# Four edits to the order of work in a hybrid encoder step: low halves, head operands, seven-product jobs, first gate

## The chip, the cores and the metric

The kernel runs on one core of a Trainium2 chip, as one launch. The metric is the device time of that launch in microseconds (us), less is better. The engines are named as in the profile: PE is TensorE (matmuls, PEld its weight loads), DVE is VectorE, ACT is ScalarE, POOL is GpSimd, SP is SyncE, whose queue issues nearly all DMAs.

## The reference, cut to what matters

One layer over 512 prompt tokens and 64 sample tokens. The normalised input is projected by one wide matrix into eleven pieces of 1024 columns, which feed three branches: a gated recurrence (A), differential attention (B) and attention into 256 memory tokens (M). Each branch output is gated, projected again, and the three are merged by sigmoid gates that come from the same first projection.

```
xn = rms_norm(x, g_norm)
hq, hf, hi, za, dq, dk, dv, zb, mq, zm, gr = split_columns(xn @ w_in)
...                       # y_a: recurrence, y_b: differential attention, y_m: memory attention
gates = sigmoid(gr).reshape(B, T, 3, D_MODEL)
h = 0
for n, (y_n, z_n) in enumerate(((y_a, za), (y_b, zb), (y_m, zm))):
    h = h + gates[:, :, n] * ((y_n * silu(z_n)) @ w_branch[n])
y = x + h @ w_out
```

## The kernel before, in words

**Products.** Every projection is done in pieces of 256 output columns, called jobs. A float32 product is made of three fp32r products: weights and tokens are each split into a high half (a copy in fp32r, made by ScalarE) and a low half (the rest, a subtraction), and high x high, high x low and low x high are added up in PSUM. A job comes in three kinds. "N" puts tokens on the rows of the result (`mms`, L333 for the prompt, L346 for the sample). "T" puts output columns on the rows (`mms`, L297): four groups of 24 matmuls of 288 tokens, 96 in all. "S" (`strassen`, L460) gives the same result as "T" from seven block products in place of eight, 84 matmuls; for that it needs sums of weight blocks (L249, VectorE), seven split units of weights where the others have four, and sums of partial results (L425, L433 on VectorE, L440 on ScalarE).

**Weights.** `load_next` issues the DMA of half a job's weights into one of three `raw` buffers (L187, SP). `conv_next` issues the splits in the order of `plan`: the high half on ScalarE (L215), the low half (L218) on the engine that `lo_engine` names. Until the sums of S jobs exist (`XS`, made at the end of the recurrence) every second low half of T and N jobs goes to POOL, 44 in all; later all go to VectorE. Eight units of split weights are kept (`NUNIT`), and units are converted while the job before runs.

**The order of the work** is written by hand. `seq` lists the jobs; `run_jobs` walks through them, and after each 12 matmuls or so calls `weave`, one step of the clock by which everything else is issued: `later(n, fn)` runs `fn` n steps on, and each generator that was pushed (`push(gen, rate)`) advances by `rate` pieces per step. Every engine takes its instructions in the order in which they were issued, so a wait holds all that stands behind it.

- `rest` (L1921 on) normalises and transposes the input blocks beside the first job: `prep_x` scales a block, `prep_xT` transposes it on TensorE (L618) and splits it (L622, L625; for the sample also `xs2`, L628, L629).
- `hgrn` is the recurrence of one head: scans and reciprocals on VectorE, products on VectorE and POOL (L835, `Kb` among them), then small matmuls (L912 to L971).
- `mem_head` is the memory attention, and `diff_pair` the differential attention of two heads. Its table `todo` puts pieces on steps: for head j, with `y0` 0 or 14, the operands `build_q`, `build_k`, `build_s` at steps `y0`, `y0 + 1`, `y0 + 2` (transposes L1115, high halves L1125 and L1142, low halves L1129 and L1145, copies to the other 64 rows L1146 and L1147), score products (L1204, L1205, then maximum L1212 and exponential L1220) from `y0 + 5`, then `combine`, `transp` (L1243, L1246) and `values` (L1276). Pairs 0 to 2 run at rate 1, the last at `LAST_B` = 1.5. `finish_heads` then normalises, transposes (L768, after L759) and gates a head; `y_out` stores it, `y_splits` loads it again and splits it (L675, L679) for the branch projection.
- `gr_jobs(n)` are the gate jobs of branch n, S jobs whose tanh (L1682) is stored to DRAM (`g_store`). `branch_jobs(n)` project a branch's heads (T jobs). Branch 0 stores its result to DRAM (`r_d`). Branch 2 loads that, its own gate and gate 0, applies gate 0 (L1709) and adds its own gated result (L1707, L1711); branch 1 does the same with the sum and gate 1, and splits the result for the last projection.

**`seq` from the pairs on**, before the change: `dq`, `dk` (N) of pair 0; `dv`, gate, `z` (S) of pair 0, gate; pair 1's three N jobs; then the two S jobs `z` of pairs 1 and 2 side by side; pair 2's three N jobs; the S job `z` of pair 3 and the last gate job `gr[11]` side by side; pair 3's three N jobs; branch 2; branch 1; the last projection. Pair 2 is pushed with `z` of pair 3, pair 3 with branch 2. The first job of branches 2 and 1 begins with the heads that are there and waits for the rest; heads of branch 1 are split only while about `spare` slots or more are free, and branch 2's slots are given back at the start of branch 1 (`y_free(2)`).

Of the kernel before, what the change touches and what calls it, by code (L numbers as in the profile page):

```python
# [66 lines left out]
def encoder_step(ctx, tc, ins, outs):  # L67
# [99 lines left out]
    lo_n = [0]  # L167

    def lo_engine():

        lo_n[0] += 1
        return ge if lo_n[0] % 2 == 0 and not XS else ve
# [311 lines left out]
    def later(n, fn):  # L484

        due.setdefault(tick[0] + n, []).append(fn)
# [616 lines left out]
    def diff_pair(hp, A):  # L1103
# [177 lines left out]
        for j, y0 in ((0, 0), (1, 14)):  # L1281
            for d, fn in enumerate((build_q, build_k, build_s)):
                todo.setdefault(y0 + d, []).append((4, fn, (j,)))
            for i in range(NT + 1):
                for rank, (d, fn) in enumerate(((D_VAL, values), (D_TR, transp), (D_COMB, combine), (0, lambda j, i: scores(j, i, 0)),
                                                (1, lambda j, i: scores(j, i, 1)))):
                    todo.setdefault(y0 + 5 + 2 * i + d, []).append((rank, fn, (j, i)))
# [357 lines left out]
    g0 = {}  # L1645
    r_d = [drams.tile([P, TT], F32, name=f"r_{b}") for b in range(8)]
    h_d = {n: [drams.tile([P, TT], F32, name=f"h{n}_{b}") for b in range(8)] for n in (2,)}
    g_d = {n: [drams.tile([P, TT], F32, name=f"g{n}_{b}") for b in range(8)] for n in range(3)}
# [19 lines left out]
    def gr_jobs(n):  # L1668

        out = []  # L1670
        for c in range(4):
            def dst(blk, half, c=c):
                b = 2 * c + blk
                if b not in gates:
                    gates[b] = slots.get()
                return gates[b][:, half * TH : (half + 1) * TH]

            def evac(blk, half, src, c=c, dst=dst):
                b = 2 * c + blk
                sl = slice(half * TH, (half + 1) * TH)  # L1680
                g = dst(blk, half)
                se.activation(out=g, in_=src, func=AF.Tanh, scale=0.5)  # L1682
                seen[b] = seen.get(b, 0) + 1
                if seen[b] == 2:
                    seen.pop(b)
                    later(2, lambda: g_store(n, b))
            seen = {}
            j = Job(w_in, GR + n * D + c * CW, "S", evac, f"gr{n}")
            j.dst = dst
            out.append(j)  # L1690
        return out

    def branch_jobs(n):
        out = []
        for c in range(4):
            def evac(blk, half, ps, c=c):
# [11 lines left out]
                if n == 2 and half == 0:  # L1708
                    ve.scalar_tensor_tensor(out=h2[b][:, 0:TT], in0=g0[b][:, 0:TT], scalar=1.0, in1=h2[b][:, 0:TT], op0=ALU.add, op1=ALU.mult)  # L1709
                    slots.put(g0.pop(b))  # L1710
# [20 lines left out]
            if n:  # L1731
                def pre(c=c):
                    def load(b):
                        h_load(h_d[2] if n == 1 else r_d, b)
                        gates[b] = g_load(n, b)
                        if n == 2:
                            g0[b] = g_load(0, b)
                    if c == 0:
                        load(0)
                    load(2 * c + 1)  # L1740
                    if c < 3:
                        later(5, lambda: load(2 * c + 2))
                before(j, pre)
# [47 lines left out]
    LAST_A, LAST_B = 1.1, 1.5  # L1791
# [41 lines left out]
    gr = gr_jobs(0) + gr_jobs(2) + gr_jobs(1)  # L1833
# [38 lines left out]
    seq += [DJ[0][2], gr[9], DJ[0][3], gr[10]] + DJ[1][0:3] + [DJ[1][3], DJ[2][3]] + DJ[2][0:3] + [DJ[3][3], gr[11]] + DJ[3][0:3]  # L1872
# [4 lines left out]
    seq += br  # L1877
    br = branch_jobs(1)
    br[0].gate = lambda: None
    before(br[0], lambda: y_free(2))  # L1880
# [10 lines left out]
    with tc.manual_schedule():  # L1891
# [24 lines left out]
        def rest():  # L1916
# [8 lines left out]
            yield  # L1925
            prep_xT(3)
            yield
            yield
            prep_xT(4)
            put(*gn)  # L1930
            yield
# [37 lines left out]
```

## Time and profile before

| | |
|---|---|
| median of 3 runs | 1121.91 us (1118.06 to 1123.19) |
| the profiled execution | 1122.42 us |
| its span, first to last instruction | 1120.7 us |
| TensorE's mean granted clock | 0.992 |
| ACT busy, POOL busy | 573.3 us, 233.4 us |
| HBM read, written | 114.74 MB, 34.47 MB |

A row of busy time by stage holds: from and to, length, then for each engine its busy time and number of instructions, TensorE's granted clock, the busy share of the DMA engines and GB/s. A row of waits holds: who waited (engine, tile, line), who ended it, the total, how often, the longest. A piece of the chain holds its start, its length and what it was. A row of a group holds the line, engine, operation, tiles, shapes and number, then busy time and the mean of one in ns, then the idle time before it. Line numbers are those of the kernel before.

### The profile page before, as it was taken

How to read it: one execution, taken by the hardware profiler on the slowest of the kernel's cores; microseconds unless marked ns; L12 is line 12 of the kernel's file. 1: busy time of each engine (PE TensorE's matmuls, PEld its weight loads, DVE VectorE, ACT ScalarE, POOL GpSimd, SP SyncE). 2: the span in 40 equal slices, each digit the busy share in tenths (PEclk: the TensorE clock that was granted, in tenths of full speed). 3: DMA queues.
4: the chain of work that ended last, by engine and by line, in shares of the span. 5: the costliest groups of instructions: out<-in, count | busy, mean ns of one | idle time of the engine just before them, and what ended most of it. 6: DMA issues, size and time to landing. Idle time of an engine off the chain costs nothing.

```text
span 1120.7 us, 22273 instructions
## 1 busy us (share of the span) xinstructions
PE 1091.1 (97%) x8685; PEld 1073.7 (96%) x8685; DVE 789.9 (70%) x1603; ACT 573.3 (51%) x1355; POOL 233.4 (21%) x406
## 2 busy tenths in 40 slices
PE   8999999999999999999999999999998998899998
PEld 6999999999899999999999999998998998898998
DVE  5479495876835666688784679679769878776641
ACT  6443323333233466568675557757757855643220
POOL 2435455453610000000000210140221131010000
PEclk9999999999999999999999999999999999999999
DMA  5442233224323656754435333223223536465442
GB/s 190 151 147 71 78 102 96 63 85 130 121 93 120 216 192 205 226 191 157 145 120 185 102 121 112 74 96 114 66 80 115 174 102 225 165 215 183 145 141 65
DMA packets 127930, 150.66 MB, mean 134 GB/s; under 512 B 7731, under 2 KB 104655, under 8 KB 127825
## 3 DMA queue, kind: packets, MB, share of 16 engines
q1 hardware_dynamic: 127820, 149.24, 41.2%
q8 instruction: 68, 1.11, 0.4%
q14 instruction: 38, 0.30, 0.1%
q10 hardware_dynamic: 4, 0.00, 0.0%
HBM read 114.74 MB, written 34.47 MB: 133 GB/s over the span
## 4 chain that ended last, share of the span: by engine, by line
PE 81%; DVE 9%; DMA 3%; ACT 3%; issue 2%; POOL 1%; SPq 1%; DVEq 0%; ACTq 0%; POOLq 0%
PE d L297 26%; PE d L333 25%; PE d L460 14%; PE d L346 4%; DVE wl L218 3%; PE abank L1276 1%; DMA raw<-in_w_in_dram 1%; PE abank L1530 1%; DVE slot L249 1%; PE abank L1243 1%; PE abank L912 1%; PE abank L1597 1%; PE abank L1205 1%; ACT wh L215 1%; PE abank L948 1%
## 5 line engine op out<-in xcount | busy, mean ns | idle before, releaser
L333 PE MATMUL d<-wh,xh 128*128 128x256 f32 x768 | 223.4, 291 | 0.8 <-ACT xh L622 0.8
L333 PE MATMUL d<-wh,xl 128*128 128x256 f32 x768 | 218.4, 284 | 0.5 <-DVE xl L625 0.3
L333 PE MATMUL d<-wl,xh 128*128 128x256 f32 x768 | 218.2, 284 | 0.0
L218 DVE TENSOR_TENSOR wl<-raw,wh 128x512 fp32r<-128x512 f32 x240 | 171.8, 732 | 54.2 <-ACT wh L215 52.8
L215 ACT ACTIVATE wh<-raw 128x512 fp32r<-128x512 f32 x284 | 168.2, 622 | 4.8 <-DMA raw<-in_w_in_dram 4.4
L297 PE MATMUL d<-slot,wh 128*128 128x288 f32 x768 | 159.3, 301 | 3.6 <-DVE slot L679 3.5
L333 PEld LDWEIGHTS d<-wh,xh 128*128 128x128 f32 x768 | 147.9, 193 | 2.0 <-ACT xh L622 1.2
L333 PEld LDWEIGHTS d<-wh,xl 128*128 128x128 f32 x768 | 147.9, 193 | 1.0 <-DVE xl L625 1.0
L333 PEld LDWEIGHTS d<-wl,xh 128*128 128x128 f32 x768 | 148.2, 193 | 0.5
L460 PE MATMUL d<-XS,wh 128*128 128x288 f32 x640 | 132.7, 301 | 0.0
L297 PEld LDWEIGHTS d<-slot,wh 128*128 128x128 f32 x768 | 126.0, 192 | 5.5 <-DVE slot L679 4.6
L297 PE MATMUL d<-xh,wh 128*128 128x288 f32 x384 | 116.7, 304 | 0.0
L297 PE MATMUL d<-slot,wl 128*128 128x288 f32 x384 | 114.7, 299 | 0.0
L297 PE MATMUL d<-xh,wl 128*128 128x288 f32 x384 | 113.1, 294 | 0.0
L297 PE MATMUL d<-xl,wh 128*128 128x288 f32 x384 | 113.1, 294 | 0.0
L460 PEld LDWEIGHTS d<-XS,wh 128*128 128x128 f32 x640 | 103.7, 190 | 0.4
L460 PE MATMUL d<-XS,wl 128*128 128x288 f32 x320 | 95.3, 298 | 0.0
L218 POOL TENSOR_TENSOR wl<-raw,wh 128x512 fp32r<-128x512 f32 x44 | 64.4, 1467 | 70.3 <-ACT wh L215 70.3
L460 PE MATMUL d<-xh,wh 128*128 128x288 f32 x240 | 72.7, 303 | 3.9 <-ACT slot L440 2.9
L140 POOL TENSOR_SCALAR rsn<-ssn 128x16 f32<-128x16 f32 (+4 forms) x28 | 7.4, 264 | 329.0 <-ACT slot L1064 250.8
L297 PEld LDWEIGHTS d<-slot,wl 128*128 128x128 f32 x384 | 73.5, 191 | 0.0
L297 PEld LDWEIGHTS d<-xh,wh 128*128 128x128 f32 x384 | 72.1, 188 | 0.5
(324 smaller groups left out, 2596.1 us busy)
## 6 DMA issues: line engine op xcount, KB each, us to landing
raw<-in_w_in_dram SPq DMA_DIRECT2D x104, 512.0 KB
raw<-in_w_branch_dram SPq DMA_DIRECT2D x24, 512.0 KB
raw<-in_w_mkv_dram SPq DMA_DIRECT2D x16, 512.0 KB
out_dram<-slot SPq DMA_DIRECT2D x31, 256.0 KB
g<-slot SPq DMA_DIRECT2D x24, 288.0 KB
slot<-g SPq DMA_DIRECT2D x24, 288.0 KB
y<-slot SPq DMA_DIRECT2D x20, 288.0 KB
slot<-y SPq DMA_DIRECT2D x20, 288.0 KB
```

What stands on the lines that cost most here:

```text
L215: se.activation(out=u.hi, in_=src, func=AF.Copy)
L218: (eng or lo_engine()).tensor_tensor(out=u.lo, in0=src, in1=u.hi.bitcast(F32), op=ALU.subtract)
L249: e.tensor_tensor(out=v, in0=a, in1=b, op=ALU.add)
L297: pe.matmul(out=ps[:, 0:TH], lhsT=w[:, k % 4, :], rhs=x(k)[:, sl], start=(n == 0), stop=(n == 23))
L333: pe.matmul(out=ps[:, t * CW : (t + 1) * CW], lhsT=x(k)[:, sl], rhs=w[:, k % 2, :], start=(n == 0), stop=(n == 23))
L346: pe.matmul(out=ps[:, 0:CW], lhsT=st[:, k, :], rhs=w[:, k % 2, :], start=(n == 0), stop=(n == 15))
L460: pe.matmul(out=ps, lhsT=w[:, k, :], rhs=x(k), start=bool(first and n == 0), stop=stop, skip_group_check=True)
L912: pe.matmul(out=a1[o0 : o0 + 64, (c % NT) * P + 32 * i : (c % NT) * P + 32 * i + 32], lhsT=Kb[:, c * KP + i * P + r0 : c * KP + i * P + r0 ...
L948: pe.matmul(out=a4[:, c * P : (c + 1) * P], lhsT=kET[:, c * P : (c + 1) * P], rhs=vt(c), start=True, stop=True)
L1205: pe.matmul(out=b[:, 0:n], lhsT=QA[:, i * P : (i + 1) * P], rhs=KL[:, 0:n], start=False, stop=True)
L1243: pe.transpose(pt[:, b * P : (b + 1) * P], e[:, b * P : (b + 1) * P], ident)
L1276: pe.matmul(out=st["o", j][:, i * P : (i + 1) * P], lhsT=aT[:, b * P : (b + 1) * P], rhs=A["v", t][:, c : c + P], start=(b == 0), stop=(b ...
```

## The change

Four things are edited.

1. **Low halves.** POOL takes every second low half among the first 16 only (`LO_GE`), 8 in place of 44; 36 go to VectorE. In `rest` the transposes of input blocks 3 and 4 (the sample) stand one and two steps earlier.
2. **Head operands.** `build_q`, `build_k`, `build_s` stand at `y0`, `y0 + 2`, `y0 + 4`, the scores from `y0 + 7`; `LAST_B` is 1.25 in place of 1.5. `y0` of the second head stays 14.
3. **Jobs.** The S job `z` of pair 2 moves between pair 2's `dk` and `dv`. The last gate job `gr[11]` becomes a T job (`kinds`) and stands between branch 2 and branch 1; `y_free(2)` moves to it, with `early_y(1, 6)`, which lets branch 1's heads be split while some 6 slots are free.
4. **First gate.** When a gate job of branch 0 has its first half, the stored result of branch 0 is loaded (`h_load`); two steps after the second half `gated` applies the gate on VectorE, and the product is stored (`h_d[0]`). Gate 0 is no longer stored. Branch 2 loads that product and its own gate alone, and has no L1709.

```
+    LO_GE = 16
...
-        return ge if lo_n[0] % 2 == 0 and not XS else ve
+        return ge if lo_n[0] % 2 == 0 and lo_n[0] <= LO_GE else ve
...
-                todo.setdefault(y0 + d, []).append((4, fn, (j,)))
+                todo.setdefault(y0 + 2 * d, []).append((4, fn, (j,)))
...
-                    todo.setdefault(y0 + 5 + 2 * i + d, []).append((rank, fn, (j, i)))
+                    todo.setdefault(y0 + 7 + 2 * i + d, []).append((rank, fn, (j, i)))
...
+    def gated(b):
+        g = gates.pop(b)
+        ve.scalar_tensor_tensor(out=h2[b][:, 0:TT], in0=g[:, 0:TT], scalar=1.0, in1=h2[b][:, 0:TT], op0=ALU.add, op1=ALU.mult)
+        slots.put(g)
+        later(1, lambda: h_store(h_d[0], b))
...
+                if n == 0 and seen[b] == 1:
+                    h_load(r_d, b)
                 if seen[b] == 2:
                     seen.pop(b)
-                    later(2, lambda: g_store(n, b))
+                    later(2, lambda: g_store(n, b) if n else gated(b))
...
-    LAST_A, LAST_B = 1.1, 1.5
+    LAST_A, LAST_B = 1.1, 1.25
...
-    gr = gr_jobs(0) + gr_jobs(2) + gr_jobs(1)
+    gr = gr_jobs(0) + gr_jobs(2) + gr_jobs(1, "SSST")
...
-    seq += [DJ[0][2], gr[9], DJ[0][3], gr[10]] + DJ[1][0:3] + [DJ[1][3], DJ[2][3]] + DJ[2][0:3] + [DJ[3][3], gr[11]] + DJ[3][0:3]
+    seq += [DJ[0][2], gr[9], DJ[0][3], gr[10]] + DJ[1][0:3] + [DJ[1][3]] + DJ[2][0:2] + [DJ[2][3], DJ[2][2], DJ[3][3]] + DJ[3][0:3]
...
-    seq += br
+    seq += br + [gr[11]]
+    before(gr[11], lambda: (y_free(2), early_y(1, 6)))
...
             prep_xT(2)
             prep_x(4)
             yield
-            yield
             prep_xT(3)
-            yield
             yield
             prep_xT(4)
             put(*gn)
+            yield
+            yield
             yield
             prep_hgrn()
```

What moves, at three places, shows in the order of the instructions. First POOL, at the last head of the recurrence (`Kb` are its products that feed TensorE, `rs` the scale of the head before, `wl` a low half of weights). Before:

```order
L835 TENSOR_TENSOR X_357_3776<-Bl_3773,U_3770 128x4
L218 TENSOR_TENSOR wl_3919<-raw_3660,wh_3918 128x512
L140 TENSOR_SCALAR rs_361_3874<-ss_360_3873 128x4
L141 TENSOR_TENSOR rs_361_3874<-rs_361_3874,nhalf 128x4
L140 TENSOR_SCALAR rs_361_3874<-ss_360_3873 64x1
L141 TENSOR_TENSOR rs_361_3874<-rs_361_3874,nhalf 64x1
L835 TENSOR_TENSOR Kb<-slot_141_3746,U_3770 128x5x32
L835 TENSOR_TENSOR Kb<-slot_141_3746,U_3770 128x4x32
L835 TENSOR_TENSOR Kb<-slot_141_3746,c_356_3775 128x4x64
L835 TENSOR_TENSOR slot_141_3746<-slot_141_3746,Y_3772 128x576
L218 TENSOR_TENSOR wl_3970<-raw_3729,wh_3969 128x512
L921 COPY qdS<-slot_140_3745 128x64
```

And now, with lines one further on:

```order
L836 TENSOR_TENSOR X_357_3776<-Bl_3773,U_3770 128x4
L140 TENSOR_SCALAR rs_361_3874<-ss_360_3873 128x4
L141 TENSOR_TENSOR rs_361_3874<-rs_361_3874,nhalf 128x4
L140 TENSOR_SCALAR rs_361_3874<-ss_360_3873 64x1
L141 TENSOR_TENSOR rs_361_3874<-rs_361_3874,nhalf 64x1
L836 TENSOR_TENSOR Kb<-slot_141_3746,U_3770 128x5x32
L836 TENSOR_TENSOR Kb<-slot_141_3746,U_3770 128x4x32
L836 TENSOR_TENSOR Kb<-slot_141_3746,c_356_3775 128x4x64
L836 TENSOR_TENSOR slot_141_3746<-slot_141_3746,Y_3772 128x576
```

The low halves, each of which needs a high half from ScalarE, no longer stand ahead of the scale and of `Kb`.

Second ScalarE, in the last pair: the key halves' copies (the last step of `build_k`) and the first exponential after them. Before:

```order
L1146 ACTIVATE slot_652_12304<-slot_652_12304 64x512
L1147 ACTIVATE slot_654_12306<-slot_654_12306 64x512
L1146 ACTIVATE slot_653_12305<-slot_653_12305 64x512
L1147 ACTIVATE slot_655_12307<-slot_655_12307 64x512
L1220 ACTIVATE slot_658_12396,zz_12354<-abank_82,mx_1317_12355 128x128
```

Now (the copies are L1147 and L1148, the exponential L1221; `wh` are high halves of weights, L747 and L751 belong to a head of the pair before):

```order
L1147 ACTIVATE slot_650_12171<-slot_650_12171 64x512
L1148 ACTIVATE slot_652_12173<-slot_652_12173 64x512
L747 ACTIVATE slot_655_12216<-slot_656_12217 128x512
L216 ACTIVATE wh_12283<-raw_12027 128x512
L216 ACTIVATE wh_12286<-raw_12095 128x512
L751 ACTIVATE slot_655_12216,ss_1292_12214<-pado_1753 64x128
L216 ACTIVATE wh_12320<-raw_12027 128x512
L1221 ACTIVATE slot_659_12323,zz_12261<-abank_85,mx_1298_12262 128x128
```

Between the last copy and the first use of the scores there is other work now.

Third TensorE, at the end of branch 2 (`d` is a job's bank, its first source the tokens, its second the weights). Before, branch 1 follows at once, on split heads (`slot`):

```order
L297 MATMUL d_13151<-slot_629_12005,wh_12819 128x288
L297 MATMUL d_13151<-slot_630_12006,wh_12819 128x288
L297 MATMUL d_13151<-slot_629_12005,wl_12820 128x288
L297 MATMUL d_13192<-slot_709_13021,wh_13010 128x288
L297 MATMUL d_13192<-slot_710_13022,wh_13010 128x288
L297 MATMUL d_13192<-slot_709_13021,wl_13011 128x288
```

Now the gate job follows, on the input (`xh`, `xl`), with work of the last heads ahead of it:

```order
L298 MATMUL d_12961<-slot_621_11789,wh_12603 128x288
L298 MATMUL d_12961<-slot_620_11788,wl_12604 128x288
L1277 MATMUL abank_84<-slot_625_11848,slot_702_12949 128x128 x2
L1277 MATMUL abank_84<-slot_632_11956,slot_702_12949 128x128 x2
L1244 MATMUL abank_81<-ident,slot_699_12914 128x128 x3
L769 MATMUL abank_83<-ident,slot_688_12734 128x128 x4
L298 MATMUL d_13007<-xh,wh_12782 128x288
L298 MATMUL d_13007<-xl,wh_12782 128x288
L298 MATMUL d_13007<-xh,wl_12783 128x288
```

The 96 matmuls of the gate job stand where the first job of branch 1 stood. That job then starts its three early groups with five heads each, where it had four.

More of the change, by code (lines that the diff above doesn't have):

```diff
@@ L1644, in encoder_step @@
     gates = {}
-    g0 = {}
     r_d = [drams.tile([P, TT], F32, name=f"r_{b}") for b in range(8)]
-    h_d = {n: [drams.tile([P, TT], F32, name=f"h{n}_{b}") for b in range(8)] for n in (2,)}
-    g_d = {n: [drams.tile([P, TT], F32, name=f"g{n}_{b}") for b in range(8)] for n in range(3)}
+    h_d = {n: [drams.tile([P, TT], F32, name=f"h{n}_{b}") for b in range(8)] for n in (0, 2)}
+    g_d = {n: [drams.tile([P, TT], F32, name=f"g{n}_{b}") for b in range(8)] for n in (1, 2)}
     def h_store(to, b):
@@ L1666, in g_load, with gr_jobs @@
         return g
-    def gr_jobs(n):
+    def gated(b):
[3 more added lines that the diff above has]
+        later(1, lambda: h_store(h_d[0], b))
+    def gr_jobs(n, kinds="SSSS"):
         out = []
@@ L1683, in evac @@
                 seen[b] = seen.get(b, 0) + 1
+                if n == 0 and seen[b] == 1:
+                    h_load(r_d, b)
                 if seen[b] == 2:
                     seen.pop(b)
-                    later(2, lambda: g_store(n, b))
+                    later(2, lambda: g_store(n, b) if n else gated(b))
             seen = {}
-            j = Job(w_in, GR + n * D + c * CW, "S", evac, f"gr{n}")
-            j.dst = dst
+            j = Job(w_in, GR + n * D + c * CW, kinds[c], evac, f"gr{n}", lhs=xT)
+            if kinds[c] == "S":
+                j.dst = dst
             out.append(j)
@@ L1707, in evac @@
                 ve.scalar_tensor_tensor(out=g[:, sl], in0=g[:, sl], scalar=1.0, in1=ps, op0=ALU.add, op1=ALU.mult)
-                if n == 2 and half == 0:
-                    ve.scalar_tensor_tensor(out=h2[b][:, 0:TT], in0=g0[b][:, 0:TT], scalar=1.0, in1=h2[b][:, 0:TT], op0=ALU.add, op1=ALU.mult)
-                    slots.put(g0.pop(b))
                 ve.tensor_tensor(out=h2[b][:, sl], in0=h2[b][:, sl], in1=g[:, sl], op=ALU.add)
@@ L1733, in load @@
                     def load(b):
-                        h_load(h_d[2] if n == 1 else r_d, b)
+                        h_load(h_d[2 if n == 1 else 0], b)
                         gates[b] = g_load(n, b)
-                        if n == 2:
-                            g0[b] = g_load(0, b)
                     if c == 0:
@@ L1876, in encoder_step @@
     before(br[1], lambda: early_y(1, 14))
-    seq += br
+    seq += br + [gr[11]]
+    before(gr[11], lambda: (y_free(2), early_y(1, 6)))
     br = branch_jobs(1)
     br[0].gate = lambda: None
-    before(br[0], lambda: y_free(2))
     seq += br
```

## The prediction, made before the changed kernel was run

> **What bounds the kernel now.** I read the busy table first, then the busy time by stage, the chain that ended last for the pace of TensorE, and last the list of who TensorE waited for, stage by stage.
>
> ```profile
> span 1120.7 us, 22273 instructions
> PE 1091.1 (97%) x8685; PEld 1073.7 (96%) x8685; DVE 789.9 (70%) x1603; ACT 573.3 (51%) x1355; POOL 233.4 (21%) x406
> ```
>
> TensorE (PE) is the bound almost everywhere. A change can win the time in which it stands or runs at a lower clock, and nothing more. The stages below are cut at the jobs: start, the recurrence (two rows), `br0` to the first gates, the attention pairs with two seven-product jobs side by side (rows 751.50 and 837.70) and their neighbours, branch 2, the first job of branch 1, the rest.
>
> ```profile
> core 0: us, PE busy (x) PEld busy (x) DVE busy (x) ACT busy (x) POOL busy (x), PEclk, DMA share, GB/s
> 0.00:32.50 32.50, 26.33 (x156) 21.94 (x157) 19.78 (x32) 19.53 (x44) 11.31 (x25) 1.00 0.56 182
> 32.50:262.90 230.40, 230.40 (x1995) 228.73 (x1994) 158.61 (x292) 82.15 (x195) 105.54 (x195) 1.00 0.31 99
> 262.90:333.90 71.00, 69.14 (x619) 67.91 (x618) 48.87 (x85) 23.38 (x49) 30.27 (x50) 0.98 0.34 110
> 333.90:475.20 141.30, 141.30 (x1107) 141.30 (x1106) 92.09 (x153) 73.14 (x157) 6.86 (x11) 1.00 0.59 191
> 751.50:781.60 30.10, 27.46 (x198) 27.08 (x197) 27.53 (x59) 21.03 (x47) 2.62 (x6) 0.94 0.38 118
> 781.60:837.70 56.10, 55.77 (x462) 55.19 (x461) 42.24 (x106) 35.44 (x89) 13.08 (x18) 1.00 0.24 76
> 837.70:867.10 29.40, 26.39 (x198) 25.68 (x197) 26.41 (x56) 20.77 (x47) 4.90 (x8) 1.00 0.34 105
> 867.10:923.00 55.90, 55.90 (x463) 55.36 (x462) 45.81 (x111) 41.12 (x101) 13.39 (x18) 1.00 0.40 134
> 923.00:1004.50 81.50, 74.65 (x539) 72.36 (x538) 65.84 (x159) 45.51 (x111) 9.16 (x20) 0.96 0.59 197
> 1004.50:1024.60 20.10, 16.47 (x103) 14.95 (x103) 13.09 (x26) 7.74 (x15) 1.34 (x3) 0.92 0.64 215
> 1024.60:1120.70 96.10, 92.09 (x738) 91.88 (x736) 42.13 (x87) 20.24 (x46) 0.00 (x0) 1.00 0.38 124
> ```
>
> Busy time hides part of the loss, since a matmul's row covers its latency too. The pace tells more, and the longest pieces of the chain give it.
>
> ```profile
> 37.64 25.65 PE d L297 x192
> 73.03 11.51 PE d L333 x96
> 84.54 1.92 PE d L346 x16
> 390.76 11.19 PE d L460 x84
> ```
>
> So a "T" job (96 matmuls at 25.65/192 = 0.1336 us) needs 12.8 us, an "S" job of seven products 11.2, an "N" job 11.51 + 1.92 = 13.4. Row 781.60 holds three N jobs (336 instructions, 40.3 us): its 126 others took 15.8 us, 0.125 each. With these prices the two rows with paired S jobs lose 30.1 - 22.4 - 30 x 0.125 = 3.95 and 29.4 - 22.4 - 3.75 = 3.25 us; branch 2 loses 81.5 - 51.3 - 155 x 0.125 = 10.8; the first job of branch 1 loses 20.1 - 12.8 - 0.9 = 6.4. That is 24.4 us in four places. Who ended the waits, for 651 to 1025 us, then two earlier lists:
>
> ```profile
> PE d L297 <- DVE slot L679: 3.5, 4, 1.1
> PE d L460 <- ACT slot L440: 2.9, 2, 1.9
> PE abank L768 <- DVE slot L759: 2.1, 3, 1.0
> PE abank L1204 <- ACT slot L1146: 2.1, 1, 2.1
> PE abank L1276 <- ACT slot L1246: 1.8, 1, 1.8
> PE abank L1115 <- ACT slot L1220: 1.8, 2, 1.0
> PE abank L1205 <- ACT slot L1147: 1.1, 1, 1.1
> PE d L460 <- DVE slot L694: 0.9, 1, 0.9
> PE abank L1243 <- DVE r L743: 0.8, 1, 0.8
> ...
> PE d L346 <- DVE xs L629: 1.5, 2, 0.7
> ...
> PE abank L912 <- POOL Kb L835: 1.3, 1, 1.3
> PE abank L920 <- POOL Kb L835: 0.4, 2, 0.2
> ```
>
> Each edit of the change has its wait in this list.
>
> **The change part by part**, against the profiled execution: 1122.4 us, that is the span and 1.7 us around it, 0.5 above the median.
>
> *x transposed earlier.* The last two blocks move up by one and two steps, ahead of 12 and 24 matmuls. The sample rows are then split before TensorE comes to them: its two waits for `xs` (1.5 us) go. Next late would be the second job's weights, which are converted beside the end of the first as now. Gain 1.5; between 0 (weights bind) and 2.
>
> *Low halves off POOL.* 36 of the 44 subtractions on POOL go to VectorE (DVE).
>
> ```profile
> L218 DVE TENSOR_TENSOR wl<-raw,wh 128x512 fp32r<-128x512 f32 x33 | 30.5, 930 | 23.0 <-ACT wh L215 22.9
> ...
> L218 DVE TENSOR_TENSOR wl<-raw,wh 128x512 fp32r<-128x512 f32 x39 | 25.7, 686 | 0.3
> ...
> L218 POOL TENSOR_TENSOR wl<-raw,wh x32: 1264/1299/2347, 61.4 to 306.4; 128x512 fp32r<-128x512 f32 x32
> ...
> POOL wl L218 <- ACT wh L215: 18.7, 4, 12.6
> ```
>
> The first row is VectorE's subtraction between 60 and 320 us, with POOL at the same work: 930 ns. The second is the same instruction from 390 to 470 us with POOL quiet: 686. VectorE gets 36 x 0.686 = 24.7 us more, and its 33 present ones give back up to 33 x 0.244 = 8.1, its other operands in SBUF some more. It has 230.4 - 158.6 = 72 us idle there, so TensorE shouldn't see it. What it sees is POOL: the products for `Kb` queue behind a subtraction that waits for ScalarE, for up to 12.6 us, and row 262.90 is idle for 1.86 us at a clock of 0.98 (another 1.4). Half or more of this 3.3 goes: gain 2, between 3.3 and a loss that is the second rival.
>
> *First gate applied at once.* Eight gate stores, eight gate loads and the loads of `r` leave branch 2; eight loads of `r` and eight stores of `h` come beside the first gate jobs, with eight VectorE instructions.
>
> ```profile
> L1709 DVE SCALAR_TENSOR_TENSOR slot<-slot,slot x8: 750/751/752, 933.4 to 1001.9; 128x576 f32<-128x576 f32 x8
> L1656 SPq DMA_DIRECT2D slot<-r x8: 320/421/611, 921.8 to 982.2; - x8
> SPq L187 <- DVE wl L218: 275.3, 58, 14.8
> ```
>
> These cost 8 x 0.75 = 6 us of VectorE beside 92.09 busy in 141.30: hidden. The load of `r` is queued on SP behind a weight load that waits for its buffer; if it lands late, the gate instruction holds VectorE, and the next weights' low halves behind it. An S job has seven weight units and the pool eight, so TensorE is one product ahead (1.6 us). I take 0; at worst 1 us in each of four jobs, 4.
>
> *S jobs apart.* The list gives 2.9 + 0.9 us to S jobs that wait for ScalarE and VectorE (L440, L694), in just these rows, with VectorE busy 27.53 of 30.10 and 26.41 of 29.40. The neighbours have it at 75% and 82%, so spread out there is room: over the four rows from 751.50 to 923.00 it works 142.0 of 171.5 us, 83%. I take those 3.8 whole and half of the remaining 3.4: 5.5. The least is 0 (first rival), the most 7.2.
>
> *Operands two steps apart, last pair at 1.25 for 1.5 steps.* In branch 2 the score products wait for key halves (L1204, L1205: 3.2 us), then values for the transposed weights (L1276: 1.8), and two more (L1115 at most 1.0, L1243 0.8): 6.8 idle, at a clock of 0.96. The halves now have five steps at 1.25, four ticks, where four steps at 1.5 gave under three, and their last copy is issued in the third. VectorE loses the 6 us of first gates here as well. I take 7.5 of the 10.8, between 3.2 and 10.8.
>
> On the clock: no wait in the list exceeds 2.1 us, and rows 751.50, 923.00 and 1004.50 still show 0.94, 0.96 and 0.92. [...]
>
> *A gate job between the branches.* Now branch 1 starts with heads not yet split.
>
> ```profile
> 1006.00 4.35 DMA slot<-y
> 1012.31 0.67 DVE slot L679
> ```
>
> Loading a head takes 4.35 us, and the first job waits four times for L679. In the new place 12.8 us of TensorE work that needs no head runs while they are fetched and split, and the slots of branch 2 are free before it. What stays is the last head's own chain. I take 5.2 of the 6.4; 0 if the last pair ends too late. As a T job it costs 12.8 - 11.2 = 1.6 more.
>
> Sum: -1.5 - 2 - 5.5 - 7.5 - 5.2 + 1.6 = -20.1; 1122.4 - 20.1 - 0.5 = 1101.8, so **1102 us**. All good ends together give 2 + 3.3 + 7.2 + 10.8 + 6.4 - 1.6 = 28.1 (1094); all bad ends leave 3.2 - 4 - 1.6 = -2.4, 1124.
>
> **Rivals.**
>
> *VectorE keeps the pair stage.* Row 751.50 says it is the engine behind the S jobs; at 83% over the whole stretch it may stall them one by one. Then that term gives 0 and branch 2 only its 3.2: -1.5 - 2 - 3.2 - 5.2 + 1.6 = -10.3, 1112. Against it: rows 781.60 and 867.10, without loss at 75 and 82%.
>
> *Slower: VectorE late in the recurrence.* Each of its subtractions there also idled for 23.0/33 = 0.70 us for ScalarE, so 36 more take up to 36 x 1.39 = 50 us. Half of the jobs there carry the scans and reciprocals; 18 on the path are 25 us, against 18.1 gained elsewhere: 1129. It decides from 0.5 us per subtraction (18.1/36). Against it: 72 us of idle VectorE, and weights that are converted a job ahead. [...]
>
> *The last pair ends late.* 1.25 for 1.5 steps over more steps, and pair 2 reaching into branch 2: branch 1 waits as before, its 5.2 gone: 1107. Against it: 12.8 us of cover.
>
> *It doesn't do what it says.* The gates' loads hold VectorE (+4), the operands gain their 3.2 alone, the S jobs 3.8, and nothing else comes: 1122.4 - 7.0 + 1.6 + 4 - 0.5 = 1120.5.
>
> **How the numbers follow.** Forecast 0.69 (own range 1094 to 1108), VectorE in the pair stage 0.14, late pair 0.08, slower 0.05, nothing 0.04. The range 1093 to 1114 takes in the first three and leaves out the last two with the edges. A measurement of this kernel tells 0.5%, 5.6 us, from no change. Faster by over that (under 1116.3): 0.91 less some edge, 0.89; slower 0.05; within 0.06.
>
> **What would show it.** Right: no TensorE wait for `xs`, none for `Kb`, none of L1204 and L1205's successors for key halves, paired-row losses under 2 us, first branch-1 job within 15 us, VectorE's subtraction near 690 ns throughout. Wrong: TensorE waits for low halves before 334 us or at 390 to 475 us, VectorE over 90% in any stretch with an S job, or waits for L440's successor as long as now.

## The result and the profile after

The changed kernel takes 1108.3 us (median of 4 runs, 1107.8 to 1108.9); the kernel before took 1120.9 beside it. The ratio is 0.9889, with a 95% interval of 0.9864 to 0.9915: 12.6 us are gained, where 20.1 were forecast. The sign of the forecast was right; its time is 6 us too low, and that is nearly all in one term of the sum.

The head of the profile after; the profiled execution took 1107.84 us, 14.6 less than that of before. That is 2 us more than the medians differ by: TensorE's clock fell five times in the profiled execution of before and once in this one, not counting the kernel's last microseconds. Each of these six lasts 3.41 us at a clock of 0.50 and so costs up to 1.7 us (last section).

```profile
span 1106.2 us, 22261 instructions
PE 1083.0 (98%) x8697; PEld 1068.2 (97%) x8697; DVE 783.7 (71%) x1627; ACT 571.9 (52%) x1350; POOL 182.8 (17%) x370
```

Busy time by stage, in the columns of the first table of the prediction. The rows are: the start; the last part of the recurrence; z of pair 1 with pair 2's `dq`; pair 2's `dk`; pair 3's `dk`; branch 2; the moved gate job; the first job of branch 1.

```profile
0.00:31.96 31.96, 25.64 (x157) 21.66 (x157) 18.05 (x32) 19.74 (x44) 9.92 (x18) 1.00 0.53 169
262.20:331.10 68.90, 67.16 (x619) 66.31 (x618) 48.67 (x93) 23.40 (x49) 20.54 (x40) 1.00 0.36 113
749.60:777.20 27.60, 27.60 (x225) 27.60 (x224) 22.24 (x51) 18.52 (x42) 4.74 (x8) 1.00 0.44 138
777.20:799.00 21.80, 19.75 (x159) 18.87 (x158) 18.36 (x42) 16.93 (x40) 5.41 (x8) 1.00 0.08 25
863.90:887.10 23.20, 21.04 (x158) 20.20 (x157) 19.87 (x44) 19.23 (x44) 5.67 (x9) 0.93 0.43 135
905.70:982.30 76.60, 74.44 (x573) 73.05 (x571) 63.96 (x162) 46.22 (x116) 7.30 (x18) 1.00 0.53 175
982.30:995.90 13.60, 13.60 (x106) 13.60 (x105) 7.25 (x14) 6.54 (x15) 1.95 (x4) 1.00 0.72 235
995.90:1010.00 14.10, 13.71 (x102) 13.31 (x102) 10.17 (x21) 7.27 (x15) 0.00 (x0) 1.00 0.67 239
```

Who ended TensorE's waits from 649 to 1010 us:

```profile
PE abank L1200 <- ACT slot L1221: 3.4, 5, 0.8
PE abank L1116 <- DVE slot L1130: 2.8, 3, 1.4
PE abank L1277 <- ACT slot L1247: 1.9, 2, 1.8
PE abank L776 <- DVE slot L772: 1.1, 1, 1.1
PE abank L769 <- DVE slot L760: 0.7, 1, 0.7
PE d L298 <- DVE slot L680: 0.4, 1, 0.4
PE abank L1200 <- DVE slot L1130: 0.2, 1, 0.2
```

The waits that the change was aimed at are gone or small: none of S jobs (L441, L695 are the lines now), none for key halves, L680 at 0.4 in place of 3.5 us. But the first two rows, 6.2 us, are new, save for the 1.8 us that L1115 waited before. L1200 is the first matmul of a sample score, L1116 a transpose of head operands; neither waits for its data, but for the bank that it writes into, which an exponential (L1221) or a low half of queries (L1130) still reads. The third row of busy times shows an S job beside an N job without a loss, the fourth and fifth two N jobs that take 21.8 and 23.2 us.

The table adds the loss up by place: a job's length, less each of its matmuls at the median spacing of its kind; waits and lower clock are both in it. The pair stage is here from pair 1's `dq` to branch 2. Another choice of the medians moves the pair stage by about 1 us, the other columns by less.

| lost by TensorE, us | recurrence, last two jobs that lose | pair stage | branch 2 | gate job and first job of branch 1 |
|---|---|---|---|---|
| before | 5.9 | 9.7 | 11.6 | 6.9 |
| changed | 3.8 | 11.1 | 3.1 | 1.0 |
| forecast of the change | -2 | -5.5 | -7.5 | -5.2 |
| measured | -2.2 | +1.4 | -8.5 | -5.9 |

So the pair stage is what is missing, and it even lost a little more. Falls of the clock are in these numbers: in the pair stage one before (at 773.8 us) and one in the changed kernel (876.4), in branch 2 two before (937.6 and 964.9) and none after, in the last column one before (1016.1) and none after. At 1.7 us each that is 3.4 of branch 2's 8.5 and 1.7 of the 5.9.

### The profile page after: what moved, and what is told of

It reads as the page before. It is cut to its first block, busy times and chain, and to the rows that moved or that the text cites. A ratio compares the mean times of both kernels' runs of the same rounds, so it can differ in the third digit from the quotient of the medians.

```text
span 1106.2 us, 22261 instructions
## 1 busy us (share of the span) xinstructions
PE 1083.0 (98%) x8697; PEld 1068.2 (97%) x8697; DVE 783.7 (71%) x1627; ACT 571.9 (52%) x1350; POOL 182.8 (17%) x370
## 4 chain that ended last, share of the span: by engine, by line
PE 86%; DVE 9%; issue 2%; DMA 2%; ACT 1%; POOL 1%; SPq 0%; DVEq 0%; ACTq 0%; POOLq 0%
PE d L298 27%; PE d L334 23%; PE d L461 18%; PE d L347 3%; DVE wl L219 2%; PE abank L1277 1%; PE abank L1531 1%; PE abank L1598 1%; DVE mx L1213 1%; PE abank L1244 1%; PE abank L1206 1%; PE abank L913 1%; DVE slot L250 1%; PE abank L1205 1%; PE abank L1116 1%
## 5 line engine op out<-in xcount | busy, mean ns | idle before, releaser
L219 DVE TENSOR_TENSOR wl<-raw,wh 128x512 fp32r<-128x512 f32 x277 | 191.6, 711 | 58.4 <-ACT wh L216 57.2
L298 PE MATMUL d<-xh,wh 128*128 128x288 f32 x416 | 126.3, 304 | 0.0
L461 PE MATMUL d<-XS,wh 128*128 128x288 f32 x608 | 125.4, 299 | 0.0
L298 PE MATMUL d<-xh,wl 128*128 128x288 f32 x416 | 122.5, 294 | 0.0
L298 PE MATMUL d<-xl,wh 128*128 128x288 f32 x416 | 122.5, 294 | 0.0
L461 PEld LDWEIGHTS d<-XS,wh 128*128 128x128 f32 x608 | 97.7, 188 | 0.3
L461 PE MATMUL d<-XS,wl 128*128 128x288 f32 x304 | 90.1, 297 | 0.0
L298 PEld LDWEIGHTS d<-xh,wh 128*128 128x128 f32 x416 | 78.2, 188 | 0.5
L298 PEld LDWEIGHTS d<-xl,wh 128*128 128x128 f32 x416 | 78.2, 188 | 0.0
L298 PEld LDWEIGHTS d<-xh,wl 128*128 128x128 f32 x416 | 78.0, 188 | 0.0
L461 PE MATMUL d<-xh,wh 128*128 128x288 f32 x228 | 68.3, 300 | 0.0
```

The source lines that it names most:

```text
L219: (eng or lo_engine()).tensor_tensor(out=u.lo, in0=src, in1=u.hi.bitcast(F32), op=ALU.subtract)
L298: pe.matmul(out=ps[:, 0:TH], lhsT=w[:, k % 4, :], rhs=x(k)[:, sl], start=(n == 0), stop=(n == 23))
L461: pe.matmul(out=ps, lhsT=w[:, k, :], rhs=x(k), start=bool(first and n == 0), stop=stop, skip_group_check=True)
```

## The experiments

Two theories were held against each other for it. *Banks*: operands two steps apart push the first head's scores two steps back (from `y0 + 5` to `y0 + 7`), but the second head still starts at step 14. Its operands (14, 16, 18) now stand among the first head's last scores (15, 16), and the five small banks don't reach. *VectorE*, the prediction's first rival: it is a step behind in the whole stage, and whatever waits for it, waits there. The changed kernel's line numbers hold, unless said otherwise.

### The second head's operands behind the scores (e1)

```
-                todo.setdefault(y0 + 2 * d, []).append((4, fn, (j,)))
+                todo.setdefault(y0 + (2 * d if j == 0 else d + 2), []).append((4, fn, (j,)))
```

> The changed kernel with the second head's operands of every pair at steps 16, 17, 18 in place of 14, 16, 18; the first head's stay at 0, 2, 4, and all scores stay where they are. In the changed kernel (1108.3 us) TensorE waits 3.4 us at L1200 and 3.0 us at L1116 between 649 and 1010 us, for a bank. Theory 'banks': the second head's first transposes now stand among the first head's last scores (steps 15 and 16), and five banks don't reach; moved behind those scores, these 6.4 us go to under 2 and the time is 1102 to 1105. Theory 'VectorE': it is behind by a step there, and any bank it empties comes late; three operands in three steps make this no better, the waits stay at 5 to 8 us and the time at 1108 to 1111.

Measured: 1101.3 us (1099.8 to 1103.6), ratio to before 0.9839 (0.9813 to 0.9864), 0.7 us below the band of the first theory. The waits from 649 to 1010 us:

```profile
PE abank L776 <- DVE slot L772: 2.0, 1, 2.0
PE abank L1277 <- ACT slot L1247: 1.9, 2, 1.8
PE abank L1116 <- ACT slot L1221: 0.8, 2, 0.5
PE abank L769 <- DVE slot L760: 0.6, 1, 0.6
PE abank L1200 <- ACT slot L1221: 0.5, 1, 0.5
```

And pair 2's `dk`, which is row 777.20 of the changed kernel:

```profile
775.20:795.30 20.10, 19.43 (x157) 18.79 (x157) 17.97 (x41) 16.13 (x40) 5.81 (x8) 1.00 0.09 27
```

L1200 and L1116 wait 1.3 us in place of 6.4. VectorE does the same work in that job and is busier by share (17.97 of 20.10, 89%, against 18.36 of 21.80, 84%), yet TensorE hardly waits. This is what "banks" said, and a busy VectorE doesn't do it alone. In branch 2, where the last pair too now has its second head's operands in three steps, 5.4 us are lost in place of 3.1, with a fall of the clock (at 940.7 us) that the changed kernel's profile does not have there.

### The whole second head later, in two of the pairs (e2)

```
-        for j, y0 in ((0, 0), (1, 14)):
+        for j, y0 in ((0, 0), (1, 16 if hp in (0, 2) else 14)):
```

> The changed kernel with the whole second head of pairs 0 and 2 (operands, scores and all behind them) two steps later, operands still two steps apart; pairs 1 and 3 as they are. 'Banks': the waits in pair 0's first N job and in pair 2's dk (losses of some 1.8 and 4.0 us) go, those in pair 1's dk (2.5) stay: 1103 to 1106. 'VectorE': they stay in all three, since no work was taken away: 1107 to 1110. In both, pair 2 ends two steps later, beside branch 2, which may cost up to 1.

Measured: 1104.1 us (1102.8 to 1107.7), ratio 0.9867 (0.9839 to 0.9895). Pair 0's N job in the changed kernel, then here, then pair 2's here (`dk` of pair 3, row 863.90 of the changed kernel):

```profile
692.90:714.40 21.50, 20.08 (x167) 19.47 (x165) 14.51 (x36) 15.65 (x37) 1.32 (x5) 1.00 0.31 99
```

```profile
692.50:711.80 19.30, 19.30 (x163) 19.18 (x162) 13.97 (x34) 15.71 (x37) 1.31 (x5) 1.00 0.33 108
862.10:881.50 19.40, 19.09 (x157) 18.66 (x156) 18.29 (x41) 16.63 (x39) 5.09 (x5) 1.00 0.50 164
```

Pair 0's N job goes from 21.5 to 19.3 us and pair 2's from 23.2 to 19.4, 1.5 or so of that because the clock does not fall there, while pair 1's, untouched, stays at 21.7. The wait goes exactly where the overlap was taken out, with the operands still two steps apart.

### Low halves from VectorE to POOL (e3)

```
+        if 55 <= i <= 62:
+            return ge if lo_n[0] % 2 == 0 else ve
```

> The changed kernel with every second low half of the N jobs of pairs 1 to 3 (12 subtractions, from pair 2's dq on) on POOL in place of VectorE. It takes 12 x 0.69 = 8 us from VectorE in the stretch where it is 80 to 88% busy. 'VectorE': the bank waits in pair 1's and pair 2's dk and dv (9.2 us lost) go down by half or more: 1102 to 1105. 'Banks': they stay within 2 us: 1106 to 1109. If POOL comes too late with them, or VectorE's own subtractions go from 0.69 to 0.93 us beside it, it is slower: 1110 or more.

Measured: 1107.5 us (1106.5 to 1109.4), ratio 0.9895 (0.987 to 0.9919); L1200 and L1116 (two lines further on) still wait 3.0 and 2.2 us. This tells less than it was meant to. A job's low halves are made one job earlier, and beside pair 2's `dk` only the S job's stand, all VectorE's; so nothing was taken from VectorE at that place. At pair 3's `dk` two were. It loses 3.0 us in place of 4.0, but only because the clock does not fall there, as it does in row 863.90: its waits come to 2.5 us against 2.1 in the changed kernel, and 1.0 of them is new, for a scale that POOL now makes late.

### S jobs side by side again (e4)

```
-    ... [DJ[1][3]] + DJ[2][0:2] + [DJ[2][3], DJ[2][2], DJ[3][3]] + DJ[3][0:3]
+    ... [DJ[1][3], DJ[2][3]] + DJ[2][0:3] + [DJ[3][3]] + DJ[3][0:3]
```

> The changed kernel with the seven-product jobs of pairs 1 and 2 side by side again, as before the change; the last gate job stays between the branches, all else is as changed. It prices the term 'S jobs apart'. If the term holds as forecast, the S jobs wait again for ScalarE and VectorE and the time rises by 4 to 6: 1112 to 1114. If VectorE only moved the loss from S jobs to the N jobs behind them, the waits change place and the time stays: 1107 to 1110. If steps 14 to 18 are short of banks whichever job they lie in, the N jobs' waits stay as well.

Measured: 1108.5 us (1107.1 to 1109.0), ratio 0.9897 (0.987 to 0.9925): beside operands two steps apart, the moved S job is worth nothing. The waits in the two S jobs (750 to 780 us), then in pair 2's three N jobs (779 to 837 us):

```profile
PE d L461 <- ACT slot L441: 1.3, 1, 1.3
PE d L461 <- DVE slot L695: 0.8, 2, 0.7
PE abank L769 <- DVE slot L760: 0.4, 1, 0.4
```

```profile
PE abank L1277 <- ACT slot L1247: 1.1, 2, 0.7
```

The S jobs wait again, as forecast. But pair 1's second head, at the same steps 14, 16, 18 and with the same five banks, no longer waits at L1200 and L1116 at all: these steps now lie beside `dq`, where VectorE makes four low halves, and not beside `dk`, where it makes an S job's eleven sums and halves. So the shortage of banks costs more where VectorE is late besides.

### z before `dk` (e9)

```
-    ... [DJ[1][3]] + DJ[2][0:2] + [DJ[2][3], DJ[2][2], DJ[3][3]] + DJ[3][0:3]
+    ... [DJ[1][3], DJ[2][0], DJ[2][3], DJ[2][1], DJ[2][2], DJ[3][3]] + DJ[3][0:3]
```

> The changed kernel with one job moved: the seven-product job z of pair 2 stands between pair 2's dq and dk, in place of between dk and dv. Its weights' sums and low halves (11 VectorE instructions of 0.69 us, 7.6 us) are then made beside dq and no longer beside dk, where pair 1's second head splits its operands. All steps of the pairs stay. If the bank waits of pair 1 need a late VectorE besides the five banks, L1200 and L1116 no longer wait there (2.5 us) and the time is 1104 to 1107. If the banks alone do it, the waits only change the job, and the time is 1107 to 1110.

Measured: 1106.3 us (1105.0 to 1108.2), ratio 0.9868 (0.9846 to 0.989), in the band of the first theory. The interval overlaps that of the changed kernel (0.9864 to 0.9915), so the time alone does not tell the two apart; the waits say more. The waits of pair 2's `dq` to `dv` in the changed kernel (762 to 835 us), then here (763 to 835 us):

```profile
PE abank L1200 <- ACT slot L1221: 1.8, 3, 0.7
PE abank L1277 <- ACT slot L1247: 1.8, 1, 1.8
PE abank L1116 <- DVE slot L1130: 0.7, 1, 0.7
```

```profile
PE abank L1277 <- ACT slot L1247: 2.2, 2, 1.5
PE abank L1200 <- ACT slot L1221: 0.5, 1, 0.5
```

With the S job's sums out of the way L1116 no longer waits and L1200 once in place of three times. What stays, L1277, is of another kind: a value product that waits for its transposed weights. VectorE's lag in the changed kernel can be seen directly. This is VectorE before the release at 789.90 us for which TensorE waited (start, length, instruction):

```profile
785.52 0.68 DVE L1031 TENSOR_REDUCE ssn<-slot 128x8 f32<-128x512 f32 x1
...
786.36 0.69 DVE L1213 TENSOR_REDUCE mx<-abank 128x1 f32<-128x512 f32 x1
...
787.41 0.62 DVE L1233 SCALAR_TENSOR_TENSOR slot<-slot,cc,slot 128x384 f32<-128x384 f32 x1
787.94 0.41 DVE L1038 TENSOR_REDUCE ssn<-slot 64x4 f32<-64x256 f32 x1
788.38 1.51 DVE L1130 SCALAR_TENSOR_TENSOR slot<-abank,gdq,slot 64x512 fp32r<-64x512 f32 x2
```

No row has an idle time behind it: VectorE works without a pause, and the two instructions that give the bank back take 1.51 us together and come last.

### Operands one step apart, last pair still at 1.25 (e5)

```
-                todo.setdefault(y0 + 2 * d, []).append((4, fn, (j,)))
+                todo.setdefault(y0 + d, []).append((4, fn, (j,)))
...
-                    todo.setdefault(y0 + 7 + 2 * i + d, []).append((rank, fn, (j, i)))
+                    todo.setdefault(y0 + 5 + 2 * i + d, []).append((rank, fn, (j, i)))
```

> The changed kernel with all operands one step apart and scores from y0 + 5, as before; the last pair stays at 1.25 pieces per step. It separates the two halves of the edit on operands. 'Banks': with nothing of the second head among the first head's last scores, the N jobs of pairs 1 and 2 lose under 3 us in place of 9, and 1.4 us stay in pair 0's first N job, as before the change. In branch 2 the key halves have 4 steps at 1.25, 3.2 steps of the clock, against 2.7 before and 4 in the changed kernel. If the distance is what pays there, the waits for key halves return (2 to 4 us): 1104 to 1108 in all. If the rate alone pays, branch 2 stays at a loss near 3 us and the time is 1101 to 1103.

Measured: 1107.8 us (1104.4 to 1109.7), ratio 0.9878 (0.9852 to 0.9904). The row of branch 2 and its waits (900 to 982 us):

```profile
901.90:980.80 78.90, 74.62 (x572) 73.05 (x570) 61.75 (x155) 46.10 (x114) 7.73 (x18) 1.00 0.53 174
```

```profile
PE abank L1205 <- ACT slot L1147: 1.9, 2, 1.1
PE abank L1277 <- ACT slot L1247: 1.6, 1, 1.6
```

The key halves are waited for again, and branch 2 loses 5.5 us in place of 3.1. The pair stage loses 6.1: 3.6 less than before the change, since the S jobs are apart, and 5.0 less than in the changed kernel. Both of those profiles have a fall of the clock in the stage and this one has none; without it the differences are some 2 and 3 us. So the forecast's two terms are each there when the other is not: S jobs apart are worth 2 to 3.6 us (forecast 5.5), and the distance of two steps takes 3 to 5 from the pairs while it gives branch 2 2.4. The N jobs of pairs 1 and 2 still lose 4.8 us, where under 3 were expected.

The whole run shows less than its profile. The profiled execution was the fastest of the four (1104.4 us at a granted clock of 0.999; the slowest took 1109.7 at 0.994), and by the medians e5 is only 0.6 us from the changed kernel.

### The first gate alone (e7)

The kernel before, with edit 4 of the change and nothing else.

> The kernel before the change with the first gate alone applied at once, all else as before. By the prediction it is worth nothing where it now stands, in the gate jobs of branch 0: no loss there, and 6 us of VectorE's work and 16 transfers less in branch 2. If branch 2's losses (11 us) hang on the order of the operands, the time is 1118 to 1121; if on VectorE's and the queue's load, branch 2 loses 3 us or more less: 1114 to 1118.

Measured: 1115.6 us (1113.4 to 1120.5), ratio 0.9966 (0.9947 to 0.9984), in the band of the second theory. Branch 2 and the first job of branch 1:

```profile
921.20:998.20 77.00, 72.90 (x539) 70.81 (x538) 61.21 (x152) 46.80 (x114) 7.81 (x20) 0.98 0.57 181
998.20:1018.00 19.80, 16.45 (x102) 15.00 (x102) 12.50 (x25) 6.40 (x13) 0.79 (x3) 0.91 0.58 207
```

Branch 2 takes 77.0 us where it took 81.5; its loss goes from 11.6 to 7.1. Row 923.00 of before had VectorE at 65.84 us, here it is 61.21. In the gate jobs, where the work went, TensorE loses nothing (0.01 us in the last of them). The prediction had put this edit at nothing and the gain under the operands. One of before's two falls of the clock in branch 2 is missing here, so some 2.8 of the 4.5 us are not the clock; the medians, 1115.6 against 1120.1 beside it, differ by 4.5 as well.

### The gate job back (e6)

`gr[11]` as an S job beside pair 3's z again, `y_free(2)` back at branch 1, the rest as changed.

> The changed kernel with the last gate job as an S job beside pair 3's S job again, branch 1 straight behind branch 2, and branch 2's slots given back at branch 1's start, all as before the change. By the step 'a gate job between the branches' (5.2 gained, 1.6 paid) branch 1's first job loses 5 to 7 us again and the paired S jobs 3 to 4, a T job's 1.6 less: 1113 to 1118. Rival, it was the last pair's rate and not the cover that freed branch 1: its first job then loses under 2 us and the time is 1106 to 1109.

Measured: 1116.9 us (1116.1 to 1119.3), ratio 0.9972 (0.9961 to 0.9983). The first job of branch 1, and its waits:

```profile
996.80:1020.70 23.90, 18.64 (x110) 17.22 (x109) 15.69 (x32) 9.86 (x21) 2.62 (x4) 0.86 0.51 166
```

```profile
PE abank L769 <- DVE slot L760: 2.2, 1, 2.2
PE d L298 <- DVE slot L680: 1.6, 3, 0.9
PE d L298 <- ACT slot L676: 1.4, 1, 1.4
```

The job takes 23.9 us, against 20.1 before the change and 14.1 in the changed kernel. With the last pair slower and two steps longer, branch 1 would be worse off than before; L769 is a last head's transpose, still due in this job. The moved gate job covers that. The clock fell twice in the job (0.86), 3.4 us of its loss. The S jobs side by side lose some 2 us, where 3 to 4 were expected. The rival of the rate is out.

### Low halves back on POOL (e8)

```
-        return ge if lo_n[0] % 2 == 0 and lo_n[0] <= LO_GE else ve
+        return ge if lo_n[0] % 2 == 0 and not XS else ve
```

> The changed kernel with POOL at every second low half until the sums of S jobs exist, 44 in place of 8. By the step 'low halves off POOL' the recurrence's last head waits for Kb and loses 1.5 to 2.5 us more: 1109 to 1111, VectorE's subtraction back at some 930 ns before 320 us. If the waits for Kb have another cause (they did not go in the changed kernel, 1.7 us), the time stays: 1107 to 1109.

Measured: 1109.6 us (1108.6 to 1110.2), ratio 0.9897 (0.988 to 0.9914). VectorE's subtraction between 60 and 320 us, here, then in the changed kernel:

```profile
L219 DVE TENSOR_TENSOR wl<-raw,wh 128x512 fp32r<-128x512 f32 x33 | 30.7, 935 | 23.0 <-ACT wh L216 22.9
```

```profile
L219 DVE TENSOR_TENSOR wl<-raw,wh 128x512 fp32r<-128x512 f32 x67 | 48.1, 742 | 26.4 <-ACT wh L216 26.1
```

The subtraction goes back to 935 ns, and the first of the two jobs loses 1.7 us in place of 1.0. TensorE's waits for `Kb` are the same in both, 1.3 and 0.4 us. So the edit is worth 0.7 us in these two profiles, and not by these waits; by the times alone the two kernels can't be told apart. The other 1.5 us of the table's first column are the clock of one job, which changes from one execution to the next (last section).

### Distance only in the last pair, z before `dk`, and both (e10, e11, e12)

```
+                todo.setdefault(y0 + (2 * d if j == 0 else d + 2 if hp < 3 else 2 * d), []).append((4, fn, (j,)))
```

> The changed kernel with the second head's operands of pairs 0 to 2 at steps 16, 17, 18, and those of the last pair at 14, 16, 18 as changed, so two steps apart only beside branch 2. With the second head late in all four pairs TensorE lost 5.4 us in the pair stage and 5.4 in branch 2; the changed kernel 11.1 and 3.1. If the two stages don't touch each other, 5.4 + 3.1 comes out and the time is 1098 to 1101; if branch 2's loss comes from where pair 2 ends, it stays at 1100 to 1103.

Measured for e10: 1101.8 us (1101.4 to 1103.9), ratio 0.9836 (0.9816 to 0.9856). The pair stage loses 4.3 us and branch 2 3.1, where 5.4 and 3.1 were expected, but the time is 0.8 us above the band and not to be told from e1's. So no time shows that the wider distance beside branch 2 pays once the second heads of the other pairs start late.

e11 adds the seq of e9 to e10. e12 is the changed kernel again, on the same chip.

> The two edits that helped, together: pairs 0 to 2 with the second head's operands at steps 16, 17, 18, the last pair as changed, and z of pair 2 between pair 2's dq and dk. With the first alone TensorE still lost 3.9 us in pair 2's dq to dv, with the second alone 4.0 where the changed kernel lost 5.5. If they are two causes, some 1.5 us more go: 1099 to 1101. If the second only helped where banks were short, it adds nothing: 1101 to 1103.

> The changed kernel once more, on the same chip as the run before it, for a direct comparison: 1107 to 1109 under any theory.

Measured for e11: 1100.1 us (1099.7 to 1100.3), ratio 0.9807 (0.9789 to 0.9826); for e12: 1108.6 us (1107.7 to 1109.2), 0.9881 (0.9858 to 0.9904). e11 is 8.5 us faster than the changed kernel beside it, with intervals far apart, and 22 us faster than the kernel before. It lies in the band of two causes, but its interval and e10's overlap, so the 1.5 us that the second cause should bring are not shown. All four runs have a granted clock of 1.000. The longest of its waits from 649 to 1003 us is

```profile
PE abank L1277 <- ACT slot L1247: 2.7, 2, 2.0
```

and L1116 and L1200 wait 0.3 us each. The losses in one table (us), with the falls of the clock that lie in the three columns:

| | pair stage | branch 2 | gate job, branch 1's first | falls of the clock |
|---|---|---|---|---|
| e1 second head late | 5.4 | 5.4 | 0.1 | 1, 1, 0 |
| e2 pairs 0, 2 late | 7.1 | 3.3 | 0.1 | 0, 0, 0 |
| e4 S jobs paired | 10.8 | 3.0 | 1.0 | 1, 0, 0 |
| e5 one step | 6.1 | 5.5 | 0.0 | 0, 0, 0 |
| e7 first gate alone | 9.5 | 7.1 | 6.6 | 1, 1, 1 |
| e9 z before `dk` | 9.6 | 2.9 | 1.1 | 1, 0, 0 |
| e10 | 4.3 | 3.1 | 1.0 | 0, 0, 0 |
| e11 | 4.0 | 3.1 | 1.1 | 0, 0, 0 |

## Why the prediction was right and where it was wrong

- **The bound and the places.** TensorE bound the kernel, and the four places held the loss; all that changed, changed there. That carried the sign.
- **x transposed earlier, -1.5.** The waits for `xs` are gone. But the first job's products began at 11.07 us, where they began at 9.95 in the profile of before, since the first weights landed 1.1 us later: ScalarE began on their high halves at 7.87 us, before at 6.73, and its split of the input's first block stands behind them (10.43, before 9.30). The second job begins at 31.96 in place of 32.54, so 0.6 came. e7 has the old order, began as late (10.94), and its second job stands at 31.9 as well: when the first weights are late, the sample's split is in time anyway. e8 has the new order, began at 10.04, and was done at 30.9. The edit is worth up to 1.7 us, when the first weights come early.
- **Low halves, -2.** The size came out at 2.2, but by a wrong way: the waits for `Kb` stayed whole. 0.7 is the edit's; 1.5 was the clock. The slower rival is out: TensorE's waits up to 649 us name no low half of weights.
- **First gate, 0.** Right where it now stands, wrong on where it left: 4.5 us in branch 2, alone on the kernel before, 1.7 of them a fall of the clock less. The step said that 6 us of VectorE leave branch 2, and then counted them among the operands' 7.5.
- **S jobs apart, -5.5.** This is the step that failed. The waits for L440 and L694 did go, as read; and e5's profile shows 2 to 3.6 us gained by it. But another edit, the one on the operands, changed the ground: operands two steps apart put the second head's transposes among the first head's last scores, and the N jobs paid 3 to 5 back. The prediction counted the waits that go and priced the two edits each by itself, without setting steps 14, 16, 18 against 15, 16 and five banks. Its sign for this, VectorE over 90% beside an S job, pointed the wrong way: the S job of pair 1 had 11.21 of 12.40 us and lost nothing.
- **Operands, -7.5.** 8.5 came, of which about 4.5 are the first gate's and 2.4 the distance's (e5). The remaining 1.6 is no more than one fall of the clock: before had two in branch 2, e7 one, e5 and the changed kernel none. Nothing that stands out of the noise is left for the rate, and no run tried it by itself.
- **Gate job, -5.2 + 1.6.** 5.9 and 1.6: right. One fall of the clock less is in the 5.9. Without the moved job the changed kernel lost 10.0 us there (e6), so the rival "the last pair ends late" was true of the pair, and the cover that spoke against it held.
- **Rival "VectorE keeps the pair stage" (1112).** Half right in its outcome: the pair stage gave nothing. Its cause was not the one: with VectorE's work unchanged, e1, e2 and e10 won 4 to 7 us there by moving steps (a fall of the clock less is in e2's and e10's). What VectorE has to do at those steps decides how much the same steps and the same five banks cost (e4, e9), but it needs no full engine: in row 692.90 VectorE worked 14.51 of 21.50 us, and TensorE still waited 1.4 us at L1200 and L1116, gone in e2. That the number of banks is what is short is read from these waits; no run gave the pairs a sixth bank.
- **The clock.** The prediction saw 0.94, 0.96 and 0.92 beside waits of at most 2.1 us, and took losses by the pace, which has the clock in it. Row 863.90 of the changed kernel shows 0.93 with no wait over 1.4 us. The 6 us that the forecast was too low by are missing in the term of the S jobs and not at the clock.
- **Size.** The term that failed is 6.9 us of the sum (5.5 forecast, 1.4 the other way); the rest of the 20.1 came within 1 us each, with help from the clock: 1.5 of the low halves' 2.2, 3.4 of branch 2's 8.5 and 1.7 of the gate job's 5.9 are falls of the clock that the profile of before had and this one had not. The first of these was luck, for e12 has that fall again.

## What to carry to other kernels

When steps of one chain are spread out, write down what then stands at the same steps of the next chain, and count the buffers that both hold; the wait that is removed at one end can return as a wait for a bank at the other, under the name of whichever engine read the bank last (here ScalarE's for 3.4 us, VectorE's for 2.8). Price two edits that act on the same stretch together, and spend a distance only where it is waited for: here two steps apart gave 2.4 us beside the last branch and took 3 to 5 beside the pairs. A share of busy time, even the 90% that VectorE had here beside an S job without a loss (11.21 of 12.40 us), says little about an engine; its order against the releases that TensorE needs does. Before the losses of two profiles are compared, count the falls of the clock in each, up to 1.7 us apiece here.

## What was not expected of the hardware

TensorE's clock fell after waits of no more than 1.3 us, and not each time. The changed kernel ran twice with a profile; in both TensorE's only waits between 295 and 318 us are those for `Kb`, 1.3 and 0.2 us. The rows from 303 to 311 us, in the first execution and in e12:

```profile
303.00:307.00 4.00, 3.75 (x54) 3.46 (x55) 1.18 (x6) 0.00 (x0) 2.27 (x4) 1.00 0.18 67
307.00:311.00 4.00, 4.00 (x36) 4.00 (x35) 0.77 (x2) 0.87 (x2) 0.00 (x0) 1.00 0.00 0
```

```profile
303.00:307.00 4.00, 3.78 (x46) 3.44 (x47) 1.18 (x6) 0.00 (x0) 2.13 (x4) 0.68 0.16 57
307.00:311.00 4.00, 4.00 (x33) 4.00 (x33) 0.32 (x1) 0.81 (x2) 0.00 (x0) 0.89 0.00 0
```

The same program with the same waits ran these 8 us at 1.00 once and at 0.68 and 0.89 the other time, and the job took 21.60 and 23.07 us: 1.5 us. Of the 14 profiled executions 8 show a clock below 1 from 295 to 319 us (0.86 in e6, 0.93 in the others), with either number of low halves on POOL.

The falls of before and of the changed kernel are of one size. These are the 3.4 us before the fall in pair 3's `dk` of the changed kernel, and the fall:

```profile
873.00:876.40 3.40, 1.46 (x10) 1.02 (x8) 3.28 (x8) 2.32 (x6) 3.23 (x3) 1.00 0.30 87
876.40:879.80 3.40, 3.18 (x15) 3.18 (x16) 3.27 (x8) 2.57 (x7) 0.61 (x2) 0.50 0.32 90
```

In the profiles of before and of the changed kernel every fall ahead of the kernel's last microseconds, five and one, lasts 3.413 us at 0.50. Those of before begin at 306.1, 773.8, 937.6, 964.9 and 1016.1 us, which are 137, 48, 8 and 15 times 3.413 us apart. The 0.93 and 0.86 above come to 1.7 and 3.4 us of 24, as much as one such fall and two. In the 3.41 us ahead of each of the six TensorE was busy for 0.35 to 0.55 of the time, never wholly idle. The stretch from 821.8 us in the changed kernel, at 0.48, was followed by no fall, so this share alone does not decide; what does was not tried here. The runs of one kernel differ in their clock as well: beside e5 to e8, the fastest of 19 runs of the kernel before took 1115.3 us at a clock of 0.997, the slowest 1123.8 at 0.991. For a reader of these profiles it means that 1.5 us at one place, as in the job of the rows from 303 us, can be chance; a whole fall, 3.413 us at 0.50, comes to 1.7.
